# A two-layer diffusion backbone on one core: modulation sums and rotary products moved to PSUM, the third token part started later, and another layout for the second attention's keys and queries

## The chip, the cores and the metric

The kernel runs on one core of one Trainium2 chip. The metric is the device time of one execution in microseconds (us). A core has five engines with a queue of instructions each: TensorE (matmul; in the profile PE, and PEld for its weight loads), VectorE (DVE), ScalarE (ACT), GpSimd (POOL) and SyncE (SP), which here issues nearly all DMA transfers. Matmuls write to PSUM, which has eight banks of 128 partitions x 512 floats. In the profile, "L237" is line 237 of the kernel.

## The reference

There are 1024 latent tokens and 256 context tokens of width 1024, and two layers. For each layer, a conditioning vector gives shift, scale and gate (the modulation), once for the latent tokens and once for the context:

```
m = silu(cond) @ w + b                      # (1024) @ (1024 x 3072): shift, scale, gate
h = rms_norm(x, norm_g) * (1 + scale) + shift
x = x + gate * mixer(h)
```

The first layer's mixer has two attentions with eight query heads and two key heads each: A is global, with an RMS norm of queries and keys; B has a window of 128 tokens on either side and a sink per head. The queries and keys of the latent tokens are rotated in both:

```
x1, x2 = x[0::2], x[1::2]
out = interleave(x1 * cos - x2 * sin, x1 * sin + x2 * cos)
```

The second layer's mixer has a convolution over tokens (31 taps, with gates and a layer norm) and the second attention D: eight heads, each query looking at a neighbourhood in a 16 x 64 grid with a table of biases, and at the context. Every mixer ends in a projection of width 1024, and the result is a final RMS norm of the latent tokens.

## The kernel before

**Precision.** Values are split into a high and a low part, and each product is three matmuls (`mm3`: high x high, high x low, low x high, L337 to L339). The splitting is `split`: a cast on ScalarE (L315) and a subtraction on GpSimd or VectorE (L318).

**Tokens.** They come in three parts, `CHUNKS`: the 256 context tokens, and two parts of 512 latent ones. In the projections they are ten blocks of 128, of which blocks 0 and 1 are context, 2 to 5 the second part and 6 to 9 the third part.

**Opening.** A string, `PLAN`, gives the order by hand. Its letters are pieces of work: `a`, `b`, `c` quarter steps of modulation halves on TensorE (`mod_half`), `v` and `V` one half on VectorE (`mod_half_v`), digits the loads of a token part, `w` weights, `n` the sum of squares of the next token part (`norm_x`), `r` the broadcast of its inverse root (`norm_bc`), `H` and `h` the making of the normed and modulated h (`h_part`, which runs `make_h`, L325 to L331). In the string, the third part's `n`, `r`, `h` are the last three letters. Work in the opening is placed while `solo` is true, and then `bank` hands out projection banks in turn from two tags, `pp` and `mx`, of two banks each.

**The rest of the modulation.** The matrices of the first layer's gate and all of the second layer's are too many for the plan. They are done in halves of 512 columns by `mod_half_v`, in the background: the generator `mods` goes one step on at each `tick`, which `proj_qkv` and `proj_gate` call three times in a block of projections. A step loads or takes a slice `w` of 128 x 512 weights and adds `w` x conditioning to one sum per condition (L232 for the first product, L237 for the others; eight products per half). At the end, TensorE sums over the partitions (L243, tile `trm`) and VectorE adds the bias (L244). While `solo` holds, all products are on VectorE; later ScalarE and GpSimd do some. The background work has a lower priority (`LATE`).

**First attention's projections.** `proj_qkv(u, w)` makes four query heads, a key head and a value head for one of four head groups: u of 0 and 1 belong to A, 2 and 3 to B. The groups run in the order 2, 3, 0, 1. It goes through five pairs of blocks. Each block's 24 matmuls fill a bank of 384 columns, `pq`: 320 of queries and keys and 64 of values. ScalarE copies it to `pc` (L849). After two blocks, for A the norm follows, then the values are split and stored (L865 to L867), and the pair is rotated (L873 twice and L875 on VectorE, L877 on GpSimd). `qk_tail` then transposes a block (L885, tile `trk`), splits it (`qs`) and stores it. `proj_gate` makes the gate path. The first group (u of 2) runs alone, the next ones are woven in between the tiles of the attention of the group ahead.

**Second layer.** `d_proj(i)` projects for the head pair i of attention D: queries, keys, values and gate. Queries and keys are stored to `QD` and `KD` in DRAM in a high and a low part, with 128 partitions that hold two heads of 64. `load_head` and `load_q` bring them back for one head: the keys as high part on partitions 0 to 63 and low part on 64 to 127 of `KAt`, the queries as high part twice in `QH` and low part in `QL`. These loads, the bias tables (`bm`, `bs`), values (`Vt`) and the weights (`wr`, L348) share SP's queue. `d_proj(0)` runs beside the convolution, `d_proj(1)` beside the layer norm, and `d_proj(2)` and `d_proj(3)` are woven into attention D.

The order on each engine's queue is set when the program is built, by priorities in the order of the program and a model of the time; in the run each queue keeps its order and waits for semaphores.

Of the kernel before, what the change touches and what calls it, by code (L numbers as in the profile page):

```python
# [10 lines left out]
F32 = mybir.dt.float32  # L11
# [7 lines left out]
P = 128  # L19
# [34 lines left out]
PCB = 3  # L54
MODP = ((), (1, 3, 6))
# [26 lines left out]
PLAN = 'pavaa0vabvnabbvabrbbwcVHcccw1Ch2nrhnrh'  # L82
# [14 lines left out]
def tile_kernel(ctx: ExitStack, tc: tile.TileContext, a, out):  # L97
# [11 lines left out]
    mk, mwp, hold, layer = [0], [None], [0], [0]  # L109
    sts, pvs = [], []  # L110

    def bank(tag, name):
        if tag == "pp" and solo[0]:
            turn[0] += 1
            tag = ("pp", "mx")[turn[0] // 2 % 2]
        return ps.tile([P, 512], F32, tag=tag, name=name, bufs=BUFS[tag])
# [93 lines left out]
    def mod_half_v(pool, l, part, j, conds):  # L210
# [3 lines left out]
        accs = [pool.tile([P, 512], F32, tag=tag, name=nm("macc"), bufs=bufs) for _ in conds]  # L214
        pre = []
        for dk in range(DK):
# [13 lines left out]
            for q, t in zip(conds, accs):  # L230
                if dk == 0:
                    VE.tensor_scalar(t, w, csil[:, dk, q : q + 1], None, op0=ALU.mult)  # L232
                elif dk in MODP[q] and not solo[0]:
                    SC.activation(w, w, AF.Identity, scale=csil[:, dk, q : q + 1])
                    GP.tensor_tensor(t, t, w, op=ALU.add)
                else:
                    VE.scalar_tensor_tensor(t, w, csil[:, dk, q : q + 1], t, op0=ALU.mult, op1=ALU.add)  # L237
# [139 lines left out]
    def load_k(k, ks):  # L377
        KA, KB = Ks[k % len(Ks)]
        for s_ in range(2):
            SY.dma_start(KA[s_ * 64 : (s_ + 1) * 64, :].bitcast(F32), ks[:, s_])  # L380
        return KA, KB
# [299 lines left out]
    with ExitStack() as p0x:  # L681
# [6 lines left out]
        with tc.tile_pool(name="st0", bufs=1, reuse_waits="tile") as st0:  # L688
# [31 lines left out]
            def norm_bc(c, acc):  # L720
                n = CHUNKS[c][1]
                return run(rstd_steps(st0, [acc], n, "st"))[:, :n]
# [11 lines left out]
            for ev in PLAN:  # L734
# [24 lines left out]
                elif ev == "r":  # L759
                    bcs.append(norm_bc(len(bcs), accs[len(bcs)]))  # L760
# [6 lines left out]
            mwp[0] = None  # L767
        ap = p0x.enter_context(tc.tile_pool(name="p0", bufs=1, reuse_waits="tile"))
# [12 lines left out]

        tails = []
# [52 lines left out]

        def proj_qkv(u, w):
            wh, wl = w or load_w0("ev_qkv", u, 384)
            for jp in range(5):
                pc = ap.tile([P, 2, 384], F32, tag="pc", name=nm("pc"), bufs=PCB)
                for jj in range(2):  # L840
                    j = 2 * jp + jj
                    pp = bank("pp", nm("pq"))
# [6 lines left out]
                    SC.copy(pc[:, jj, :], pp[:, 0:384])  # L849
# [3 lines left out]
                t2 = ap.tile([P, 2, 5, 64], F32, tag="rt2", name=nm("rt2"), bufs=2)  # L853
                if u < 2:
                    SC.activation(t2, p5, AF.Square)
# [12 lines left out]
                if jp > 0:  # L868
# [52 lines left out]
        solo[0] = False  # L921
# [26 lines left out]
    QD = [dram(f"QD{i}", [P, 2, 2, 512]) for i in range(4)]  # L948
    KD = [dram(f"KD{i}", [P, 2, 12 * P]) for i in range(4)]
# [196 lines left out]
    with ExitStack():  # L1146
# [77 lines left out]
        def d_proj(i):  # L1224
            wsrc = (wp, WB)
            wh, wl = load_w(wsrc[0], a["od_d"], i * 512, 256, 256, wsrc[1])
            for c in (1, 2):
# [8 lines left out]
                for s_ in range(2):  # L1236
                    SY.dma_start(QD[i][:, s_, :, o : o + 256],
                                 sp[:, s_, :].rearrange("p (h q) -> p h q", h=2).bitcast(F32))
            for c in (1, 2, 0):
                t0, n = CHUNKS[c]  # L1240
                pp = yield from proj1(wh, wl, 1, c)
                if c == 0:
                    sp = pair("spk")
                    split(pp[:, :n], sp[:, 0, :n], sp[:, 1, :n], "s", "v")
                    SY.dma_start(KD[i][:, :, 0:n], sp[:, :, :n].bitcast(F32))
# [6 lines left out]
                if c == 2:  # L1252
                    for s_ in range(2):
                        SY.dma_start(KD[i][:, s_, 256:], sk2[:, s_, :].bitcast(F32))
# [74 lines left out]
        def load_head(hd):  # L1329
            i, e = divmod(hd, 2)  # L1330
            ds = slice(e * 64, (e + 1) * 64)
            heads[hd] = load_k(hd, KD[i][ds])

        def group1(gi, hd, hf):
# [4 lines left out]
            def load_q(QH, QL):  # L1339
                SY.dma_start(QH[0:64, :].bitcast(F32), QD[i][ds, 0, hf])  # L1340
                SY.dma_start(QH[64:128, :].bitcast(F32), QD[i][ds, 0, hf])
                SY.dma_start(QL[0:64, :].bitcast(F32), QD[i][ds, 1, hf])
# [381 lines left out]
```

## Time and profile before

| | |
|---|---|
| median of 3 runs | 1522.37 us (1521.3 to 1523.64) |
| profiled execution | 1517.21 us, span 1515.3 us |
| mean granted TensorE clock | 0.978 |
| busy TensorE, VectorE, GpSimd, ScalarE | 95%, 72%, 54%, 50% |
| DMA | 213.15 MB, mean 141 GB/s |

The profile is of one execution. The span is from its first to its last instruction. A busy time is the time in which an engine executed at least one instruction; a wait is idle time of an engine, put down to the instruction or transfer that ended it. The granted clock is the TensorE clock relative to full speed. Windows give these in stretches of the span. The stages by time are: the opening with the first group's projections, to about 140; projections woven into the first attention, to about 500; the attention with the first output projection, to about 880; the convolution with the second layer's first projections, to about 1105; then the layer norm and attention D, and the end from about 1450.

### The profile page before, as it was taken

The page shows a single profiled execution, that of the slowest core. Times are in us where ns is not written, and L with a number is a line of the kernel's source. Part 1 is how long each engine was busy: PE and PEld are TensorE (multiplying, and loading weights), DVE is VectorE, ACT ScalarE, POOL GpSimd, SP SyncE. Part 2 cuts the span into 40 slices and gives each one's busy share as a digit, 9 for nine tenths or more (in the row PEclk, how much of TensorE's full clock was granted, in tenths as well). Part 3 has the DMA queues.
Part 4 walks back from the last instruction along what each step waited for, and adds up shares of the span by engine and source line. Part 5 has one row for each costly group of instructions (what it writes and reads, how often), then busy time and mean ns, then how long its engine had stood idle before and what let it go on. Part 6 is the DMA issues. An engine that isn't in the chain of part 4 may idle for free. (4 is left out here: it accounts for less than half of the span.)

```text
span 1515.3 us, 22054 instructions
## 1 busy us (share of the span) xinstructions
PE 1435.6 (95%) x7054; PEld 1169.1 (77%) x7054; DVE 1094.9 (72%) x2096; ACT 757.0 (50%) x1541; POOL 821.0 (54%) x757
## 2 busy tenths in 40 slices
PE   7879989999999999999999989999999999999997
PEld 2879967886789678778888768888778878878777
DVE  5899898589957667555477775999936667668764
ACT  3721354445453666665445664543434355555563
POOL 3361464365645686776545665755543333354665
PEclk9999999999999999999999989999999999999998
DMA  9558235523541123652111112312395667788723
GB/s 350 207 174 253 75 120 171 156 66 98 170 140 59 38 81 116 197 169 63 43 45 46 60 53 87 93 59 80 130 313 188 215 189 207 242 264 234 196 68 112
DMA packets 180588, 213.15 MB, mean 141 GB/s; under 512 B 17004, under 2 KB 133944, under 8 KB 180472
## 3 DMA queue, kind: packets, MB, share of 16 engines
q1 hardware_dynamic: 173808, 200.16, 42.2%
q10 hardware_dynamic: 6664, 11.57, 2.4%
q8 instruction: 56, 0.92, 0.2%
q14 instruction: 60, 0.49, 0.1%
HBM read 151.64 MB, written 60.03 MB: 140 GB/s over the span
## 5 line engine op out<-in xcount | busy, mean ns | idle before, releaser
L318 POOL TENSOR_TENSOR pl<-pf,ph 128x512 fp32r<-128x512 f32 (+3 forms) x321 | 391.3, 1229 | 277.4 <-ACT ph L315 227.6
L318 POOL TENSOR_TENSOR wl<-wr,wh 128x256 fp32r<-128x256 f32 (+2 forms) x253 | 194.2, 785 | 141.5 <-ACT wh L315 113.8
L506 ACT ACTIVATE pf<-st 128x512 f32<-128x512 f32 x284 | 167.4, 597 | 178.5 <-PE st L498 127.4
L315 ACT CAST ph<-pf 128x512 fp32r<-128x512 f32 (+3 forms) x364 | 205.9, 578 | 24.9 <-PE ov L437 12.8
L337 PE MATMUL p<-hh,wh 128*128 128x512 f32 x448 | 178.1, 400 | 0.7 <-ACT wh L315 0.7
L339 PE MATMUL p<-hh,wl 128*128 128x512 f32 x448 | 175.0, 399 | 3.1 <-POOL wl L318 3.0
L338 PE MATMUL p<-hl,wh 128*128 128x512 f32 x448 | 176.2, 395 | 0.0
L315 ACT CAST wh<-wr 128x256 fp32r<-128x256 f32 (+2 forms) x260 | 102.0, 404 | 132.9 <-DMA wr<-in_od_d_dram 29.4
L436 PE MATMUL ov<-ph,Vt 128*128 128x512 f32 (+3 forms) x364 | 142.2, 391 | 13.3 <-DVE y L660 8.2
L494 PE MATMUL st<-QH,KAt 128*128 128x512 f32 (+3 forms) x364 | 140.0, 386 | 13.2 <-ACT pf L506 9.6
L438 PE MATMUL ov<-pl,Vt 128*128 128x512 f32 (+3 forms) x364 | 142.3, 392 | 4.7 <-POOL pl L318 2.7
L437 PE MATMUL ov<-ph,Vt 128*64 128x512 f32 (+3 forms) x364 | 139.3, 383 | 0.0
L498 PE MATMUL st<-QL,KBt 68*128 68x512 f32 (+3 forms) x364 | 134.6, 379 | 0.3 <-DVE QL L407 0.3
L1163 DVE SCALAR_TENSOR_TENSOR cps<-U,taps,cps 128x512 f32<-128x512 f32 x184 | 124.3, 749 | 0.0
L618 DVE TENSOR_REDUCE mp<-mx 128x1 f32<-128x512 f32 x128 | 85.5, 684 | 37.9 <-PE mx L617 37.2
L237 DVE SCALAR_TENSOR_TENSOR macc<-mw,csil,macc 128x512 f32<-128x512 f32 x107 | 95.6, 913 | 21.1 <-DMA mw<-in_mod_w_dram 20.1
L339 PEld LDWEIGHTS p<-hh,wl 128*128 128x128 f32 x448 | 84.6, 189 | 24.6 <-POOL wl L318 3.6
L337 PEld LDWEIGHTS p<-hh,wh 128*128 128x128 f32 x448 | 84.5, 189 | 19.1 <-ACT wh L315 0.9
L338 PEld LDWEIGHTS p<-hl,wh 128*128 128x128 f32 x448 | 84.6, 189 | 18.4
L436 PEld LDWEIGHTS ov<-ph,Vt 128*128 128x128 f32 x364 | 71.3, 196 | 30.9 <-issue 7.1
L438 PEld LDWEIGHTS ov<-pl,Vt 128*128 128x128 f32 x364 | 71.0, 195 | 30.5 <-POOL pl L318 7.7
L494 PEld LDWEIGHTS st<-QH,KAt 128*128 128x128 f32 x364 | 68.9, 190 | 31.1 <-ACT pf L506 15.6
(270 smaller groups left out, 3487.9 us busy)
## 6 DMA issues: line engine op xcount, KB each, us to landing
mw<-in_mod_w_dram SPq DMA_DIRECT2D x34, 512.0 KB, 5.8
Q<-qs SPq DMA_DIRECT2D x40, 256.0 KB, 2.5
QH<-Q SPq DMA_DIRECT2D x80, 128.0 KB, 2.8
bm<-in_d_bm_dram SPq DMA_DIRECT2D x16, 540.0 KB, 5.5
wr<-in_od_d_dram SPq DMA_DIRECT2D x64, 128.0 KB, 2.9
mw<-in_mod_w_dram SPq DMA_DIRECT2D x28, 256.0 KB, 3.1
wr<-in_ev_qkv_dram SPq DMA_DIRECT2D x32, 192.0 KB, 3.6
KAt<-KD SPq DMA_DIRECT2D x16, 384.0 KB, 6.2
```

The lines of the kernel that those rows point to most:

```text
L315: SC.copy(hi, src)
L318: (GP if leng == "g" else VE).tensor_tensor(lo, src, hi.bitcast(F32), op=ALU.subtract)
L337: PE.matmul(o, lh, rh, start=first, stop=False)
L338: PE.matmul(o, lh, rl, start=False, stop=False)
L339: done[0] = PE.matmul(o, ll, rh, start=False, stop=last)
L436: PE.matmul(o, V[:, 64:192], ph, start=(t == 0), stop=False)
L437: PE.matmul(cut(g.ov[0:64], q0, n), V[:, 0:64], ph, start=False, stop=False)
L438: pvs.append(PE.matmul(o, V[:, 64:192], pl, start=False, stop=(last and g.sink is None)))
L494: sts.append(PE.matmul(sf, KA[:, cs], cut(g.QH, q0, n), start=True, stop=False))
L498: PE.matmul(sf, KB[0:68, cs], cut(g.QL[0:68], q0, n), start=False, stop=True)
L506: SC.activation(pf[:, :n], st[:, :n], AF.Exp, scale=1.0 if g.bias else SCALE)
L1163: VE.scalar_tensor_tensor(pc, uc, w, pc, op0=ALU.mult, op1=ALU.add)
```

## The change

- `mod_half_v` puts the running sums of the first four halves of the background modulation (`PSH`) into PSUM banks of the tag `mx`, one per condition. The last of the eight products reads the bank and writes the sum in SBUF. While these may be used, the new flag `sums` keeps the projections on the two `pp` banks.
- The third token part's three steps leave `PLAN` and are run inside the first group's `proj_qkv`: `n` ahead of block 0, `r` ahead of block 2, `h` ahead of block 3 (`LASTN`).
- For the groups of B, blocks 2 to 9 are rotated one by one in a new function `rope`, which reads the projection's bank in place of a copy; ScalarE copies only the 64 value columns.
- `QD` and `KD` hold each head's parts in the order in which they are needed on 128 partitions, with the high part of the queries stored twice. Loading takes fewer transfers, storing takes more.

```
 PCB = 3
+PSH = 4
...
-PLAN = 'pavaa0vabvnabbvabrbbwcVHcccw1Ch2nrhnrh'
+PLAN = 'pavaa0vabvnabbvabrbbwcVHcccw1Ch2nrh'
+LASTN = (0, 2, 3)
...
+    sums, made_v = [False], [0]
...
-        if tag == "pp" and solo[0]:
+        if tag == "pp" and solo[0] and not sums[0]:
...
         accs = [pool.tile([P, 512], F32, tag=tag, name=nm("macc"), bufs=bufs) for _ in conds]
+        runs = accs
+        if mwp[0] is None:
+            made_v[0] += 1
+            if made_v[0] <= PSH:
+                runs = [ps.tile([P, 512], F32, tag="mx", name=nm("mrun"), bufs=BUFS["mx"]) for _ in conds]
...
-            for q, t in zip(conds, accs):
+            for q, t, r_ in zip(conds, accs, runs):
                 if dk == 0:
-                    VE.tensor_scalar(t, w, csil[:, dk, q : q + 1], None, op0=ALU.mult)
+                    VE.tensor_scalar(r_, w, csil[:, dk, q : q + 1], None, op0=ALU.mult)
...
-                    VE.scalar_tensor_tensor(t, w, csil[:, dk, q : q + 1], t, op0=ALU.mult, op1=ALU.add)
+                    VE.scalar_tensor_tensor(t if dk == DK - 1 else r_, w, csil[:, dk, q : q + 1], r_, op0=ALU.mult, op1=ALU.add)
...
         KA, KB = Ks[k % len(Ks)]
-        for s_ in range(2):
-            SY.dma_start(KA[s_ * 64 : (s_ + 1) * 64, :].bitcast(F32), ks[:, s_])
+        SY.dma_start(KA.bitcast(F32), ks)
...
             mwp[0] = None
+            sums[0] = True
...
+        third = [lambda: accs.append(norm_x(2)), lambda: bcs.append(norm_bc(2, accs[2], ap)), lambda: h_part(range(DK))]
...
+        def rope(pp, pc, jp, jj):
+
+            j = 2 * jp - 2 + jj
+            t2 = ap.tile([P, 640], F32, tag="rt2", name=nm("rt"), bufs=2)[:, 0:320].rearrange("p (h d) -> p h d", d=64)
+            s4 = pp[:, 0:320].rearrange("p (h i two) -> p h i two", two=2, i=32)
+            d4 = t2.rearrange("p h (i two) -> p h i two", two=2)
+            k4 = kcs[:, 1, j, :].rearrange("p (i two) -> p i two", two=2)
+            for e in range(2):
+                VE.tensor_tensor(d4[:, :, :, e], s4[:, :, :, 1 - e], k4[:, None, :, e].broadcast_to([P, 5, 32]), op=ALU.mult)
+            p5 = pc[:, jj, 0:320].rearrange("p (h d) -> p h d", d=64)
+            VE.tensor_tensor(p5, pp[:, 0:320].rearrange("p (h d) -> p h d", d=64),
+                             kcs[:, 0, j, None, :].broadcast_to([P, 5, 64]), op=ALU.mult)
+            SC.copy(pc[:, jj, 320:384], pp[:, 320:384])
+            GP.tensor_tensor(p5, p5, t2, op=ALU.add)
+
         def proj_qkv(u, w):
             wh, wl = w or load_w0("ev_qkv", u, 384)
             for jp in range(5):
+                if w:
+                    for k_, step in enumerate(third):
+                        if LASTN[k_] == 2 * jp:
+                            step()
...
                     j = 2 * jp + jj
+                    if w and jj:
+                        for k_, step in enumerate(third):
+                            if LASTN[k_] == 2 * jp + 1:
+                                step()
...
-                    SC.copy(pc[:, jj, :], pp[:, 0:384])
+                    if u < 2 or jp == 0:
+                        SC.copy(pc[:, jj, :], pp[:, 0:384])
+                    else:
+                        rope(pp, pc, jp, jj)
...
-                if jp > 0:
+                if jp > 0 and u < 2:
...
-        solo[0] = False
+        solo[0] = sums[0] = False
...
-    QD = [dram(f"QD{i}", [P, 2, 2, 512]) for i in range(4)]
-    KD = [dram(f"KD{i}", [P, 2, 12 * P]) for i in range(4)]
+    QD = [dram(f"QD{i}", [2, 192, 2, 512]) for i in range(4)]
+    KD = [dram(f"KD{i}", [2, P, 12 * P]) for i in range(4)]
...
-                for s_ in range(2):
-                    SY.dma_start(QD[i][:, s_, :, o : o + 256],
-                                 sp[:, s_, :].rearrange("p (h q) -> p h q", h=2).bitcast(F32))
+                for e in range(2):
+                    es = slice(e * 64, (e + 1) * 64)
+                    for k, s_ in enumerate((0, 0, 1)):
+                        SY.dma_start(QD[i][e, k * 64 : (k + 1) * 64, :, o : o + 256],
+                                     sp[es, s_, :].rearrange("p (h q) -> p h q", h=2).bitcast(F32))
...
-                    SY.dma_start(KD[i][:, :, 0:n], sp[:, :, :n].bitcast(F32))
+                    for e in range(2):
+                        SY.dma_start(KD[i][e].rearrange("(s d) n -> d s n", s=2)[:, :, 0:n],
+                                     sp[e * 64 : (e + 1) * 64, :, :n].bitcast(F32))
...
-                    for s_ in range(2):
-                        SY.dma_start(KD[i][:, s_, 256:], sk2[:, s_, :].bitcast(F32))
+                    for e in range(2):
+                        SY.dma_start(KD[i][e].rearrange("(s d) n -> d s n", s=2)[:, :, 256:],
+                                     sk2[e * 64 : (e + 1) * 64, :, :].bitcast(F32))
...
-            heads[hd] = load_k(hd, KD[i][ds])
+            heads[hd] = load_k(hd, KD[i][e])
...
-                SY.dma_start(QH[0:64, :].bitcast(F32), QD[i][ds, 0, hf])
-                SY.dma_start(QH[64:128, :].bitcast(F32), QD[i][ds, 0, hf])
-                SY.dma_start(QL[0:64, :].bitcast(F32), QD[i][ds, 1, hf])
+                SY.dma_start(QH.bitcast(F32), QD[i][e, 0:128, hf])
+                SY.dma_start(QL[0:64, :].bitcast(F32), QD[i][e, 128:192, hf])
```

More of the change, by code (lines that the diff above doesn't have):

```diff
@@ L718, in norm_x, with norm_bc @@
                 return acc
-            def norm_bc(c, acc):
+            def norm_bc(c, acc, pool):
                 n = CHUNKS[c][1]
-                return run(rstd_steps(st0, [acc], n, "st"))[:, :n]
+                return run(rstd_steps(pool, [acc], n, "st"))[:, :n]
             made = [0]
@@ L759, in tile_kernel @@
                 elif ev == "r":
-                    bcs.append(norm_bc(len(bcs), accs[len(bcs)]))
+                    bcs.append(norm_bc(len(bcs), accs[len(bcs)], st0))
                 elif ev == "H":
@@ L852, in proj_qkv @@
                 p5 = pc[:, :, 0:320].rearrange("p j (h d) -> p j h d", d=64)
-                t2 = ap.tile([P, 2, 5, 64], F32, tag="rt2", name=nm("rt2"), bufs=2)
                 if u < 2:
+                    t2 = ap.tile([P, 2, 5, 64], F32, tag="rt2", name=nm("rt2"), bufs=2)
                     SC.activation(t2, p5, AF.Square)
```

## The prediction

> **What bounds the kernel now.** I read the page's engine shares first, then busy time in slices of 5 us over the opening, then what TensorE waits for there, then the durations of VectorE's sums, and last the second attention's waits and transfers.
>
> ```profile
> PE 1435.6 (95%) x7054; PEld 1169.1 (77%) x7054; DVE 1094.9 (72%) x2096; ACT 757.0 (50%) x1541; POOL 821.0 (54%) x757
> ```
>
> TensorE is the bound: only 79.7 of 1515.3 us are not matmul, so an edit is worth the TensorE gaps that it closes. Where are they? The windows' columns are the stretch, its length, busy time of PE, PEld, DVE, ACT, POOL, granted clock, DMA share, GB/s.
>
> ```profile
> 80.00:85.00 5.00, 3.37 (x20) 2.76 (x19) 5.00 (x5) 0.62 (x1) 5.00 (x4) 1.00 0.24 71
> 85.00:90.00 5.00, 3.36 (x21) 3.00 (x20) 5.00 (x7) 1.76 (x4) 2.81 (x3) 1.00 0.57 184
> 90.00:95.00 5.00, 3.95 (x24) 3.66 (x23) 5.00 (x4) 1.88 (x5) 4.75 (x5) 1.00 0.47 134
> 95.00:100.00 5.00, 3.74 (x23) 3.22 (x22) 5.00 (x9) 1.30 (x3) 1.16 (x1) 1.00 0.58 171
> 100.00:105.00 5.00, 4.24 (x28) 4.25 (x29) 3.11 (x4) 0.30 (x1) 4.36 (x3) 0.79 0.89 246
> 105.00:110.00 5.00, 3.71 (x21) 2.91 (x20) 4.27 (x8) 1.46 (x5) 2.62 (x3) 0.84 0.92 288
> 110.00:115.00 5.00, 5.00 (x16) 3.91 (x16) 5.00 (x9) 1.37 (x3) 2.45 (x2) 0.69 0.61 181
> ```
>
> From 80 to 100 VectorE is busy without a break and TensorE is not; after it the clock falls for 15 us. TensorE's waits from 78 to 109 name VectorE in every row (total, times, longest):
>
> ```profile
> PE trk L885 <- DVE qs L318: 5.8, 5, 1.6
> PE trm L243 <- DVE macc L237: 0.9, 1, 0.9
> PE pq L339 <- DVE hl L329: 0.9, 1, 0.9
> ```
>
> Together 7.6 us. Why VectorE is late shows in the order of time:
>
> ```profile
> 88.97 1.84 POOL L318 TENSOR_TENSOR gl<-gr,gh 128x512 fp32r<-128x512 f32 x1 [2.19 <-ACT gh L315]
> 89.57 3.76 DVE L237 SCALAR_TENSOR_TENSOR macc<-mw,csil,macc 128x512 f32<-128x512 f32 x2
> 90.77 2.02 POOL L877 TENSOR_TENSOR pc<-pc,rt 128x640 f32<-128x640 f32 x1
> ...
> 98.57 0.74 DVE L237 SCALAR_TENSOR_TENSOR macc<-mw,csil,macc 128x512 f32<-128x512 f32 x1
> ```
>
> One sum takes 0.74 us when GpSimd is idle; two took 3.76 while GpSimd worked. The same operation elsewhere, with its running sum in PSUM (L1163, the convolution), and here with it in SBUF (L237):
>
> ```profile
> L1163 DVE SCALAR_TENSOR_TENSOR cps<-U,taps,cps x184: 743/749/752, 946.8 to 1100.6; 128x512 f32<-128x512 f32 x184
> L237 DVE SCALAR_TENSOR_TENSOR macc<-mw,csil,macc x107: 731/750/2054, 7.6 to 443.4; 128x512 f32<-128x512 f32 x107
> ```
>
> Shortest, median, longest: 743/749/752 ns against 731/750/2054. The medians are equal, only the tail differs. VectorE's groups from 70 to 112 (busy us, mean ns):
>
> ```profile
> L237 DVE SCALAR_TENSOR_TENSOR macc<-mw,csil,macc 128x512 f32<-128x512 f32 x17 | 20.7, 1233 | 0.0
> L873 DVE TENSOR_TENSOR rt<-pc,k_cs 128x320 f32<-128x320 f32 x8 | 5.6, 738 | 2.6 <-ACT pc L849 2.6
> L329 DVE SCALAR_TENSOR_TENSOR hl<-xr,modT,hh 128x512 fp32r<-128x512 f32 x4 | 5.2, 1327 | 0.0
> ...
> L875 DVE TENSOR_TENSOR pc<-pc,k_cs 128x640 f32<-128x640 f32 x4 | 3.2, 812 | 0.0
> L232 DVE TENSOR_SCALAR macc<-mw,csil 128x512 f32<-128x512 f32 x3 | 3.2, 1093 | 0.0
> ```
>
> **1. Sums in PSUM.** The first four halves after the opening's plan keep their two sums in the `mx` banks; seven of eight products of each write PSUM, the last reads PSUM and writes SBUF. At L1163's mean of 0.749, the 17 sums of 70 to 112 cost 12.7 us in place of 20.7, and three first products 2.2 in place of 3.2 (a first product in the bank priced as a sum; ends -1 and +1). VectorE gets 9 us back in a stretch where TensorE lost 7.6 to it.
>
> **2. Rotations from PSUM.** In two of the four head groups (u of 2 and 3), for blocks 2 to 9, ScalarE's copy of 384 columns shrinks to 64, and VectorE reads the projection's bank with two products of 160 and one of 320 columns per block, in place of two of 320 and one of 640 per pair. Nearest rows, one operand in PSUM and one in SBUF (by shape, whole kernel):
>
> ```profile
> L503 DVE TENSOR_TENSOR pf<-st,bs 128x256 f32<-128x256 f32 x32 | 13.4, 418 | 7.9 <-PE st L498 6.4 <-POOL pl L318 1.3
> L503 DVE TENSOR_TENSOR pf<-st,bs 128x128 f32<-128x128 f32 x16 | 4.6, 285 | 6.7 <-PE st L498 2.9 <-POOL pl L318 1.4 <-PE ov L438 1.3
> ```
>
> 133 ns per 128 columns gives 0.32 and 0.48: 1.12 us per block, 2.24 per pair, against 2 x 0.738 + 0.812 = 2.29 before. For VectorE this is even: 0, ends -2 (the four pairs at no contention) and +2 us. GpSimd has two additions of 320 for one of 640: one fixed part more, off the path.
>
> What it adds is a coupling. The bank is now free only when VectorE is through, not after a ScalarE copy, and the opening's projections have two banks in place of four, since `mx` holds the sums. One block's matmuls, first and last of 24:
>
> ```profile
> 65.46 0.42 PE L337 MATMUL pq<-wh,hh 128*128 128x384 f32 x1
> ...
> 69.54 0.34 PE L339 MATMUL pq<-wh,hl 128*128 128x384 f32 x1
> ```
>
> 4.2 us. With two banks the rotation must be over within one block. Behind two sums it ends 1.5 + 1.1 = 2.6 us after the block; a transpose's eviction ahead of it makes some 3.1 us. That fits, with 1 us to spare. I take +1 us for the blocks where it does not, ends 0 and +5 (the 5.8 us that TensorE now waits on VectorE for the transposes, most of it back under another name).
>
> **3. Third part later.** Norm, broadcast and h of the last 512 tokens, 16 + 8 + 8 VectorE and ScalarE operations on the norm and the h chain, move from before all projections to before blocks 0, 2 and 3. Nothing is added; no transfer moves (x of that part is loaded as before). Rows:
>
> ```profile
> 65.74 5.36 DVE L325 SCALAR_TENSOR_TENSOR xr<-xr,gs,bc 128x512 f32<-128x512 f32 x8 [3.21 <-PE bc L280]
> ...
> 81.67 0.44 PE L339 MATMUL pq<-wh,hl 128*128 128x384 f32 x1 [0.87 <-DVE hl L329]
> ```
>
> VectorE idles 3.2 us before this part, and TensorE waits 0.9 for its last pieces. Sums of the modulation can now come in front of it and fill the idle time, or push it back. I take 0; ends -3.2 (the idle time used) and +9 (rival D).
>
> **4. Clock.** From 100 to 115 the granted clock is 0.79, 0.84, 0.69: (0.21 + 0.16 + 0.31) x 5 = 3.4 us of lost matmul time right behind the 20 us in which TensorE was busy 72%. I let it shrink with the gaps.
> The Trainium skill's page "TensorE: Matmul & The Clock Gate", Part 1 (the clock gate), says that the clock falls after an idle window of about 3.4 us. The longest wait here is 1.6 us, so a reading of that rule by single gaps would not tie this fall to these waits. The windows show the fall behind a stretch of many short gaps; the same page's passage on micro-idling between matmul groups would allow that, and no run so far tells which. Without this tie the sum below is 2.5 us smaller.
>
> **5. Second attention.** Keys are loaded with one transfer on 128 partitions for two on 64, queries with two for three: 8 + 16 issues fewer. Stores: per head pair, queries go out in 12 transfers of 64 partitions for 4 of 128, context keys in 2 for 1: 36 more. Issues rise by 12. TensorE's waits from 1130 to 1500, the landing times (KB, median us) and the queue at one of the stores:
>
> ```profile
> PE p L339 <- POOL wl L318: 3.0, 1, 3.0
> PE mx L1383 <- DMA QH<-QD: 1.7, 2, 0.9
> ...
> PE mx L1383 <- DMA KAt<-KD: 0.5, 1, 0.5
> ```
> ```profile
> KAt<-KD SPq DMA_DIRECT2D x16, 384.0 KB, 6.2
> bs<-in_d_bs_dram SPq DMA_DIRECT2D x16, 384.0 KB, 3.7
> ```
> ```profile
> 1123.27 3.87 SPq L1237 DMA_DIRECT2D QD<-spq  x4
> 1130.65 0.35 SPq L348 DMA_DIRECT2D wr<-in_od_d_dram  x1
> ```
>
> 384 KB on 64 partitions take 6.2 us, on 128 partitions 3.7, so the loads should land sooner, but TensorE waited only 2.2 us for them in all: -2.2 is the end on that side. Behind the stores on SP's queue stand weight loads, and a weight's split held TensorE 3.0 us just there. At a pitch near 0.37 us (the second of these rows issues in 0.35) eight more issues hold the queue 3 us; SP stood idle from 1127.1 to 1130.7, which covers it once. I take +0.7 for the rest: -1.5 together, ends -2.2 and +7 (rival C).
>
> **Sum.** Of the 7.6 us 2.0 stay, since VectorE still has work in every slice (L329's 1.33 us sums have both operands in SBUF and stay slow): -5.6. Clock, in the same proportion, -2.5. Banks +1.0. Third part 0. Second attention -1.5. Behind the opening the transfers of the modulation's weights come nearer to the path; VectorE's waits from 110 to 180 have
>
> ```profile
> DVE macc L237 <- DMA mw<-in_mod_w_dram: 4.4, 4, 1.7
> ```
>
> and a faster VectorE runs into these more: I give back 1.5, ends 0 and 5. Total -7.1 us. The profiled execution took 1517.21 us (span 1515.3 and 1.9 around it): 1510.1, a factor 0.9953. The median of the runs is 1522.37, 0.34% above the profiled one; the factor on it gives 1515.2.
>
> **Rivals.** About 0.2% (3 us) is what a measurement of this kernel can tell from no change.
>
> A, more: all 7.6 and 3.4 go, and the first attention, now started with VectorE less behind, closes its own gap. The row is
>
> ```profile
> 180.00:200.00 20.00, 16.78 (x73) 11.72 (x72) 17.68 (x38) 10.41 (x24) 11.68 (x10) 0.83 0.20 61
> ```
>
> 3.2 us idle and 0.17 x 20 = 3.4 of clock. Half of these with the rest: -7.6 - 3.4 + 1 - 1.5 - 3.3 = -14.8, 1507.5. For it: the gap lies where VectorE is at 17.7 of 20. Against: that is softmax work the change leaves alone. Chance 0.16.
>
> B, the clock is not tied to the short gaps: -4.6, 1517.8. For it speaks only that each gap is short. Chance 0.08. (This is also what the clock page's rule by single windows gives.)
>
> C, no change: second attention's stores. At three of the four head pairs, 8 issues x 0.37 = 3 us go on the queue ahead of weight loads that TensorE then waits for, 9 us less the 2.2 gained: +6.8, with the opening's -5.6: +1.2, 1523.6; with one of the three hidden 1520.6. For it: the 3.0 us wait above, and a DMA share over 1 at the first of these places:
>
> ```profile
> 1120.00:1140.00 20.00, 17.03 (x86) 14.14 (x85) 6.44 (x13) 9.36 (x17) 5.87 (x7) 0.91 1.02 328
> ```
>
> Against: most weight loads there wait for a free buffer, not for the queue. It decides from two exposed places on. Chance 0.18.
>
> The Trainium skill's page "SBUF — State Buffer", section "Door 1: The DMA port swizzle", speaks against these stores: a transfer on 64 partitions reaches half of the ports. The 6.2 against 3.7 us above agree for loads; no row shows such a store of queries.
>
> D, slower: the third part comes too late. Its h work stands behind three blocks' ticks, nine of them, 18 sums x 0.749 = 13.5 us of VectorE. If the queue's order puts these first, h starts 12 us later; block 6 needs it some 3 us after the present start, so TensorE stands 9 us and then runs 3.4 us' worth of slow clock: -7.1 + 12.4 = +5.3, 1527.7. For it: TensorE waits for this part already (0.87 us). Against: VectorE idles 3.2 us right before it, and the ticks' work is put back in the order. From 7 us of delay on it eats the whole gain. Chance 0.16.
>
> **Numbers.** The forecast 1515.2 has 0.42, with its own range 1510 to 1519.3. Faster: all but 0.02 of it, A and B less 0.02: 0.62. Same: those 0.04 and most of C: 0.20. Slower: D and a rest of C: 0.18. For 8 in 10, half of A and half of D stay outside: 1506 to 1527.
>
> **What will show it.** From 80 to 100 TensorE above 18 of 20 and the trk waits under 2 us; modulation sums at 0.74 to 0.76 us in every case; a clock of 1.00 from 100 to 115; block 6 without a wait for h; no `pq` matmul that waits for the rotation; key loads at 768 KB landing in under 8.5 us; TensorE idle from 1100 to 1500 lower by 1 to 2 us. Wrong would be: waits on L329 or on the rotation in the opening, weight loads landing later behind the query stores, or an opening that ends early and an attention that starts when it did.

## The result, and the profile after

The changed kernel is faster: 1511.04 us against 1522.91 (medians of 18 runs each), ratio 0.9922 with a 95% interval of 0.9904 to 0.9940, about 12 us. A second measurement of the same two gave 0.9913 (0.9879 to 0.9947). The forecast was 1515.2, a factor of 0.9953. The total is inside its range, but the runs below show that it was not made up as the sum said.

The first profiled execution of the changed kernel took 1520.2 us (span 1518.4), 9 us above its median; that of the kernel before lay 5.7 us below its own. So stages are compared with a second profile of each. Engines of the changed kernel:

```profile
PE 1436.4 (95%) x7054; PEld 1175.0 (77%) x7054; DVE 1082.4 (71%) x2120; ACT 751.0 (49%) x1541; POOL 817.2 (54%) x765
```

TensorE is still the bound. The windows of its opening, with the columns of the windows in the prediction:

```profile
50.00:55.00 5.00, 0.43 (x4) 0.23 (x3) 5.00 (x9) 2.60 (x5) 0.64 (x1) 0.88 1.05 356
55.00:60.00 5.00, 0.00 (x0) 0.00 (x0) 5.00 (x9) 4.97 (x10) 3.35 (x4) 0.50 0.32 84
60.00:65.00 5.00, 1.61 (x8) 1.64 (x8) 5.00 (x8) 0.72 (x3) 2.54 (x2) 0.50 0.75 238
65.00:70.00 5.00, 5.00 (x17) 5.00 (x17) 5.00 (x10) 0.00 (x0) 1.01 (x1) 0.50 0.63 160
80.00:85.00 5.00, 5.00 (x35) 4.92 (x35) 5.00 (x9) 3.86 (x9) 3.27 (x4) 1.00 0.35 105
85.00:90.00 5.00, 5.00 (x31) 5.00 (x30) 5.00 (x13) 0.83 (x2) 5.00 (x5) 1.00 0.41 135
90.00:95.00 5.00, 5.00 (x33) 4.96 (x32) 5.00 (x11) 1.37 (x4) 1.89 (x3) 1.00 0.87 261
95.00:100.00 5.00, 5.00 (x34) 5.00 (x32) 5.00 (x11) 1.24 (x4) 3.43 (x4) 1.00 0.76 243
100.00:105.00 5.00, 5.00 (x36) 4.96 (x35) 5.00 (x11) 2.13 (x5) 1.31 (x2) 1.00 0.90 262
105.00:110.00 5.00, 5.00 (x38) 4.97 (x38) 4.40 (x10) 0.67 (x2) 3.44 (x4) 1.00 0.93 286
```

From 80 to 110 every gap is gone and the clock is full, more than was forecast. But there is a new hole from 50.4 to 63.4, and half the clock up to 70. The kernel before, in the first three of these windows:

```profile
50.00:55.00 5.00, 2.51 (x8) 2.29 (x9) 5.00 (x8) 4.45 (x8) 2.49 (x2) 0.67 1.07 357
55.00:60.00 5.00, 5.00 (x21) 5.00 (x20) 5.00 (x7) 3.55 (x7) 3.22 (x3) 0.65 0.10 32
60.00:65.00 5.00, 5.00 (x35) 5.00 (x34) 1.60 (x4) 0.63 (x2) 1.01 (x1) 1.00 0.61 193
```

The changed kernel in the order of time:

```profile
49.06 1.40 DVE L240 TENSOR_SCALAR mrun<-mw,csil 128x512 f32<-128x512 f32 x2
...
59.57 0.85 ACT L882 COPY pc<-pq 128x384 f32<-128x384 f32 x2
62.56 0.68 DVE L724 TENSOR_TENSOR acc<-acc,sq 128x512 f32<-128x512 f32 x1
63.39 1.84 PE L277 MATMUL trs<-ones,acc 128*128 128x2 f32 x8 [12.96 <-DVE acc L724]
```

Two projection banks are in use, and ScalarE copies blocks 0 and 1 out of them only at 59.57, behind its work for h. Block 2 has no bank, and ahead of it on TensorE's queue stands the third part's `trs`, which waits for the norm's sums, between which VectorE takes modulation sums. The copies end at 60.4, so the last 3 us of the hole are the wait of `trs`. Block 2 starts at 65.1 us; before, at 52.5.

A smaller gap follows at 111 us. TensorE waits 1.97 us there (2.50 in the second profile) for a projection bank, for the copy of the 64 value columns, which stands on ScalarE's queue behind a cast of weights that have not landed:

```profile
112.45 0.51 ACT L323 CAST wh<-wr 128x384 fp32r<-128x384 f32 x1 [1.71 <-DMA wr<-in_ev_qkv_dram]
112.87 0.20 ACT L857 COPY pc<-pq 128x64 f32<-128x64 f32 x1
...
113.13 0.51 PE L345 MATMUL pg<-hh,gh 128*128 128x512 f32 x1 [1.97 <-ACT pc L857]
```

And the gap at the first attention's start, the row of the prediction's rival A (16.78 of 20 us busy, clock 0.83), is closed:

```profile
180.00:200.00 20.00, 19.42 (x109) 17.30 (x108) 18.96 (x41) 8.78 (x22) 11.13 (x10) 1.00 0.22 66
```

VectorE's sums (shortest, median, longest) are as forecast:

```profile
L245 DVE SCALAR_TENSOR_TENSOR macc<-mw,csil,macc x51: 739/751/2155, 7.7 to 439.5; 128x512 f32<-128x512 f32 x51
L245 DVE SCALAR_TENSOR_TENSOR mrun<-mw,csil,mrun x48: 734/745/754, 51.0 to 128.7; 128x512 f32<-128x512 f32 x48
```

In the bank none of 48 is stretched; in SBUF the longest still takes 2.155 us. The Trainium skill's page "SBUF — State Buffer", section "Summary: rules for kernel authors", has VectorE with two SBUF inputs and GpSimd's SBUF reads block each other, whichever comes second; these two rows agree with it.

### The profile page after: what moved, and what is told of

Same layout as the page of the kernel before. It is cut to its first block, busy times and chain, and to the rows that moved or that the text cites. A ratio compares the mean times of both kernels' runs of the same rounds, so it can differ in the third digit from the quotient of the medians.

```text
span 1518.4 us, 22121 instructions
## 1 busy us (share of the span) xinstructions
PE 1436.4 (95%) x7054; PEld 1175.0 (77%) x7054; DVE 1082.4 (71%) x2120; ACT 751.0 (49%) x1541; POOL 817.2 (54%) x765
## 4 chain that ended last, share of the span: by engine, by line
PE 69%; DVE 11%; DMA 11%; issue 3%; POOL 2%; SPq 2%; ACT 2%; DVEq 0%; POOLq 0%; ACTq 0%
PE p L345 5%; PE p L346 5%; PE p L347 5%; PE ov L443 4%; PE ov L445 4%; PE po L345 4%; PE ov L444 4%; PE po L347 4%; PE po L346 4%; PE st L505 4%; PE st L501 4%; DMA mw<-in_mod_w_dram 3%; PE pq L345 3%; PE pq L346 2%; PE pq L347 2%
## 5 line engine op out<-in xcount | busy, mean ns | idle before, releaser
L445 PE MATMUL ov<-pl,Vt 128*128 128x512 f32 (+3 forms) x364 | 141.5, 390 | 4.2 <-POOL pl L326 2.3
L345 PE MATMUL pq<-wh,hh 128*128 128x384 f32 x256 | 88.9, 347 | 0.5 <-ACT pc L857 0.5
L347 PE MATMUL pq<-wh,hl 128*128 128x384 f32 x256 | 88.5, 346 | 0.0
```

Of the source, the lines that this page charges most:

```text
L345: PE.matmul(o, lh, rh, start=first, stop=False)
L347: done[0] = PE.matmul(o, ll, rh, start=False, stop=last)
L445: pvs.append(PE.matmul(o, V[:, 64:192], pl, start=False, stop=(last and g.sink is None)))
```

## The experiments

Nine kernels take parts of the change away or do parts alone, one adds the banks' restriction without its use, and two are the kernels themselves again. For each, the table has the ratio to the kernel before, and of its one profile, in us: the start of block 2, of the first scores (`st`), of the 31st matmul into `ov` (scores times values), and of the first into `p` (the second layer), with the stretch between the last two, "the first attention". "Order" is worked out from the traces: TensorE's matmuls from the first scores to the first `p`, as the sequence of tiles that they write (repeats merged, 1,124 to 1,186 steps); the longest common subsequence with the changed kernel's, as a share of the longer.

| kernel | ratio (95%) | block 2 | scores | ov 31 | p | first attention | order |
|---|---|---|---|---|---|---|---|
| before | 1 | 52.5 | 155.6 | 206.9 | 909.1 | 702.2 | 0.93 |
| before_again | 0.9994 (0.9970–1.0018) | 52.6 | 155.7 | 206.9 | 905.8 | 698.9 | 0.93 |
| changed | 0.9922 (0.9904–0.9940) | 65.1 | 142.5 | 201.4 | 903.7 | 702.4 | 1 |
| after_again | 0.9913 (0.9879–0.9947) | 64.4 | 142.0 | 199.4 | 902.0 | 702.6 | 1.00 |
| layout_only | 0.9934 (0.9908–0.9960) | 52.8 | 155.8 | 206.6 | 905.0 | 698.4 | 0.93 |
| no_layout | 0.9966 (0.9945–0.9986) | 65.2 | 141.7 | 201.7 | 900.8 | 699.1 | 1.00 |
| sums_late | 0.9929 (0.9902–0.9956) | 52.7 | 141.5 | 196.9 | 901.2 | 704.4 | 0.95 |
| sums_only | 1.0067 (1.0045–1.0089) | 68.1 | 143.9 | 195.7 | 914.4 | 718.7 | 0.81 |
| third_back | 0.9981 (0.9955–1.0007) | 68.7 | 143.6 | 196.5 | 913.1 | 716.6 | 0.83 |
| third_44 | 1.0009 (0.9985–1.0034) | 65.1 | 146.8 | 201.1 | 914.4 | 713.3 | 0.83 |
| no_sums | 1.0056 (1.0035–1.0077) | 52.6 | 154.7 | 207.9 | 918.6 | 710.7 | 0.82 |
| banks_only | 1.0016 (0.9997–1.0035) | 62.6 | 147.9 | 203.3 | 917.5 | 714.2 | 0.83 |
| late_third_back | 0.9977 (0.9954–1.0000) | 52.5 | 146.6 | 204.3 | 914.5 | 710.2 | 0.83 |
| no_rope | 1.0044 (1.0022–1.0066) | 64.3 | 144.0 | 200.8 | 914.4 | 713.6 | 0.83 |

Only the first `p` marks the same amount of work in all of them: 4,180 matmuls stand ahead of it. Ahead of the first scores there are 677 in the kernel before, 589 in the changed one and 654 in no_sums, and ahead of the 31st `ov` 913, 898 and 905 (860 in sums_only, 862 in third_back). So an earlier "scores" or "ov 31" is in part only less work ahead of it. "Like for like" below means corrected for these matmuls, at 0.17 to 0.23 us each for projections and scores and 0.11 for the others, spacings read from the traces: an estimate.

At first there were two theories: 1, VectorE's relief by the PSUM sums is the gain (the prediction's); 2, the two banks cost what the sums bring. (The recorded expectations number their own theories anew each time.)

**sums_only: the kernel before with the sums and the two banks alone.**

```
+            if made_v[0] <= PSH:
+                runs = [ps.tile([P, 512], F32, tag="mx", name=nm("mrun"), bufs=BUFS["mx"]) for _ in conds]
...
-        if tag == "pp" and solo[0]:
+        if tag == "pp" and solo[0] and not sums[0]:
```

> The kernel before with only the running sums of four modulation halves in PSUM (and two projection banks while they are there); rotations from the copy, the third part in the plan, the old layout. Theory 1 (the gain is VectorE's time behind GpSimd in the opening): trk waits from 78 to 109 fall from 5.8 to under 2 us, TensorE busy above 19 of 20 from 80 to 100, and 1514 to 1516 us, ratio 0.995 to 0.996. Theory 2 (most of the gain is in the second attention's loads): the opening is shorter but the end moves by under 3 us, ratio 0.998 or above. Theory 3 (the sums alone do not help, since the rotations and their copies still wait behind GpSimd): trk waits stay above 4 us.

Slower by 0.67%. Where theory 1 looked it was right: from 80 to 115 TensorE is busy without a break. But the hole is there too (a wait of 13.0 us), and the first `p` comes 7 us later than before. Theory 1 cannot stand as it was: the part that was to carry the gain costs time when alone.

**layout_only: the kernel before with the new layout alone.**

```
+    QD = [dram(f"QD{i}", [2, 192, 2, 512]) for i in range(4)]
+    KD = [dram(f"KD{i}", [2, P, 12 * P]) for i in range(4)]
...
```

> The kernel before with only the new layout of the second attention's keys and queries. Theory 1: the loads land sooner, but TensorE waited only 2.2 us for them; -1.5 us, ratio 0.998 to 1.0. Theory 2: -5 us or more, ratio 0.9965 or below. The rival of the query stores: weight loads issued later at 1130, 1190 and 1285, ratio 1.001 to 1.005.

Faster by 0.66%, several times the 1.5 us of the forecast.

**third_back: the changed kernel with the third part back in `PLAN`.**

```
-PLAN = 'pavaa0vabvnabbvabrbbwcVHcccw1Ch2nrh'
+PLAN = 'pavaa0vabvnabbvabrbbwcVHcccw1Ch2nrhnrh'
```

> The changed kernel with the third token part back in the plan, ahead of all projections. In the profile of the changed kernel TensorE stood 13.0 us at the third part's sum over partitions, ahead of block 2, and ran at half clock to 71. If the move causes this: the wait goes, block 2 starts near 52 as before, and the time falls by 5 to 10 us against the changed kernel, ratio to before 0.986 to 0.989. If the sums cause it (VectorE takes them ahead of the third part's squares): the wait stays and the ratio is near 0.992.

0.59% slower than the changed kernel: moving the third part, priced at 0, is worth 9 us in this company. The hole before block 2 is there all the same (68.7), so the move does not make it.

**third_44: the third part's last two steps ahead of block 4.**

```
-LASTN = (0, 2, 3)
+LASTN = (0, 4, 4)
```

> The changed kernel with the broadcast and h of the third part both ahead of block 4, so two blocks of projections stand in front of the sum over partitions that TensorE waited 13.0 us for. If that queue position is the cause: block 2 starts at 52 to 54, no wait above 2 us at the sum, block 6 waits for h by 0 to 5 us, net 4 to 9 us faster than the changed kernel, ratio 0.986 to 0.990. If the third part is simply late on VectorE: the wait moves to block 6 and the ratio stays near 0.992.

No faster than the kernel before, and block 2 starts at 65.1 us as in the changed one. The edit did not do what the expectation counted on: the sum over partitions `trs` still stands ahead of block 2 on TensorE's queue, with the same wait of 13.0 us, so this run says nothing on its place there.

**no_sums: the changed kernel with sums in SBUF and four banks.**

```
-PSH = 4
+PSH = 0
...
-            sums[0] = True
+            sums[0] = False
```

> The changed kernel without the PSUM sums and with the four banks for projections back in the opening; rotations, later third part and second attention's layout stay. Theory 2 (the two banks cost the opening, the relief of VectorE is worth less): block 2 starts again at 52 to 54 us instead of 65.1, the 12.96 us wait of the transposed sums is gone, the waits of 80 to 110 us come back in part (3 to 8 us), and the time is 1505 to 1511 us, ratio 0.986 to 0.991. Theory 1 (the sums in PSUM are worth their relief once the third part is late): the time is above the changed kernel's, ratio 0.994 to 1.000.

Block 2 is back at 52.6 and the hole closed, as theory 2 wanted:

```profile
50.00:55.00 5.00, 2.39 (x7) 2.16 (x8) 5.00 (x8) 4.33 (x8) 2.36 (x2) 0.65 1.05 353
55.00:60.00 5.00, 5.00 (x21) 5.00 (x21) 5.00 (x7) 3.67 (x7) 3.33 (x3) 0.67 0.10 33
```

But the kernel is 1.3% slower than the changed one. Theory 2 falls too: the 31st `ov` comes at 207.9 instead of 200.4 (some 6 us later like for like), and the first attention then takes 710.7 us. From 78 to 109 us 3.3 us of waits are back, as expected.

**banks_only: the restriction to two banks, with nothing in the others.**

```
-PSH = 4
+PSH = 0
```

> The changed kernel with the modulation sums back in SBUF and nothing in the freed banks: two banks for projections are kept in the opening. It pays the restriction and gets no relief. If the restriction makes the hole, TensorE is idle from about 50 to 63 us as in the changed kernel and the waits of 80 to 110 us are back as well: 1517 to 1524 us, ratio 0.995 to 1.000, slower than the kernel without the restriction. If the hole comes from the sums' order on VectorE, block 2 starts before 56 us and the time is within 3 us of the kernel without the restriction.

```profile
50.00:55.00 5.00, 0.35 (x4) 0.16 (x2) 4.61 (x7) 3.83 (x7) 1.86 (x2) 0.87 1.06 353
55.00:60.00 5.00, 0.00 (x0) 0.00 (x0) 5.00 (x7) 4.16 (x8) 3.20 (x3) 0.50 0.08 26
60.00:65.00 5.00, 4.11 (x16) 4.14 (x17) 4.91 (x11) 0.30 (x1) 1.75 (x2) 0.50 0.57 190
```

The hole is there without any sum in PSUM, and in no_sums, which differs by the restriction alone, it is not: the restriction makes it. Yet this kernel is 0.4% faster than no_sums. So a hole at 55 us does not decide the time.

**sums_late: two banks and PSUM sums from the fifth block on.**

```
-            if made_v[0] <= PSH:
+            if 1 < made_v[0] <= PSH:
...
-            sums[0] = True
...
             for jp in range(5):
+                if w and jp == 2:
+                    sums[0] = True
```

> The changed kernel, but the restriction to two banks and the PSUM sums begin with the fifth block of keys and queries and the second pair of modulation halves, so that blocks 0 to 3 rotate over four banks. Theory 2: block 2 starts at 52 to 55 us, most of the relief of 80 to 110 us is kept (TensorE over 4.6 of 5 us in each slice), and the time is the best of the four, 1502 to 1509 us, ratio 0.984 to 0.990. Rival (the hole moves to block 4 or to the third part's columns, wherever the two banks begin): a wait of 5 us or more shows between 70 and 95 us and the ratio stays 0.990 to 0.995.

```profile
70.00:75.00 5.00, 4.37 (x26) 4.04 (x24) 5.00 (x8) 2.40 (x5) 1.31 (x2) 1.00 0.25 95
75.00:80.00 5.00, 0.52 (x3) 0.31 (x3) 5.00 (x10) 5.00 (x10) 3.73 (x3) 0.87 0.00 0
80.00:85.00 5.00, 3.41 (x12) 3.44 (x13) 5.00 (x10) 2.84 (x8) 3.94 (x4) 0.50 0.68 188
```

The rival named there was right, though its one wait of 5 us is two, of 3.6 and 3.1: a smaller hole opens at 74 us, and VectorE is busy without a break around it. So the hole was moved and made smaller, not removed. The first scores come when they did (141.5), the 31st `ov` 3.5 us earlier than in the changed kernel, and the total is the same within the intervals.

**no_layout: the changed kernel without the new layout.** The edit is layout_only's, reversed.

> The changed kernel with the second attention's keys and queries laid out as before. Theory 2 (the layout carries most of the gain, as it did alone at 0.9934): ratio 0.997 to 1.001, 1521 to 1526 us. Theory of the prediction (the layout is worth 1.5 us): ratio 0.992 to 0.995, 1513 to 1517 us.

The layout is worth 0.44% here, between the two expectations. Up to the second layer this kernel and the changed one are the same, in TensorE's order too; what differs lies behind the first `p`.

**after_again and before_again: the two kernels, unchanged.**

> The changed kernel itself once more, for a second profile: the first fell on an execution 9 us above its median. Ratio 0.990 to 0.995. If the gain sits in the first attention, from 201 to 904 us, that stretch is 695 us or less here (702.4 in the first profile, 702.2 before). If it sits behind it (the second attention), that stretch stays at 700 to 704 us and the stretch from the first gate product of the last attention to the end is 318 to 324 us instead of 329.

> The kernel before, for a second profile: the first fell on an execution 6 us below its median. Ratio 0.998 to 1.002. If its first profile was lucky in the second attention, the 321.1 us from its first exponentials to the end are 326 to 331 us here; if it was lucky in the first attention, the 702.2 us are 706 to 712 us.

The first attention repeats within 0.2 us in the one and 3.3 in the other; neither was lucky or slow there. What varies is the second attention: from its first exponentials to the end 329.5 and 322.7 us in the changed kernel, 321.2 and 329.2 in the one before. That stretch of the kernel before, first profile and second:

```profile
1194.00:1515.00 321.00, 301.22 (x1592) 252.55 (x1590) 211.65 (x507) 172.22 (x382) 160.59 (x178) 0.97 0.63 190
```
```profile
1191.00:1520.00 329.00, 307.11 (x1592) 257.07 (x1590) 213.05 (x507) 172.00 (x382) 159.44 (x178) 0.95 0.62 186
```

The same 1592 matmuls, at a granted clock of 0.97 and 0.95, with 8 us between them.

**late_third_back: sums_late, with the third part back in `PLAN`.**

```
-PLAN = 'pavaa0vabvnabbvabrbbwcVHcccw1Ch2nrh'
-LASTN = (0, 2, 3)
+PLAN = 'pavaa0vabvnabbvabrbbwcVHcccw1Ch2nrhnrh'
+LASTN = (99, 99, 99)
```

> As the kernel whose two banks and PSUM sums begin with the fifth block, but with the third part of the columns back ahead of the blocks. Theory (each of the two edits needs the other: the third part's work on VectorE beside the blocks is what fills the 52 to 80 us there, and the relief comes later): block 2 at 52 to 53 us, block 6 at 74 to 76 us instead of 82.1, no wait over 4 us between 50 and 110 us, ratio 0.983 to 0.989. Rival (taking the third part out of the start is what shortens the way to the first scores, as in the changed kernel): the first scores are at 146 us or later and the ratio is 0.994 to 1.000.

Missed: block 6 stays late (81.9 us), the first scores come at 146.6 as its rival said, and the ratio is 0.9977.

**no_rope: the changed kernel with rotations behind the copy.**

```
-                    if u < 2 or jp == 0:
+                    if True:
...
-                if jp > 0 and u < 2:
+                if jp > 0:
```

> The changed kernel with the third unit's rotations again behind the copy in SBUF, two blocks at a time. The prediction's step (the rotations cost and bring nothing, 2 us either way): ratio 0.991 to 0.994. Rival (they free the copies of ScalarE, on which the next block's bank waits): 0.995 to 0.998, and the columns projected third take longer.

1.2% slower than the changed kernel, more than either theory allowed. Up to the 31st `ov` the two are level (200.8 and 199.4 to 201.4). Some 11 of the 19 us lost are in the first attention, 713.6 against 702.5; the rest lies behind the first `p`. From 200 to 900 us, the changed kernel (second profile) and this one:

```profile
200.00:900.00 700.00, 675.11 (x3270) 545.94 (x3269) 496.24 (x946) 381.88 (x756) 429.41 (x356) 0.98 0.33 100
```
```profile
200.00:900.00 700.00, 667.35 (x3213) 537.95 (x3212) 489.79 (x927) 375.49 (x736) 421.02 (x339) 0.98 0.32 99
```

In the same 700 us it has 57 matmuls fewer on record and TensorE idles 7.8 us more. The first place is at 226 us:

```profile
226.09 1.34 DVE L245 SCALAR_TENSOR_TENSOR macc<-mw,csil,macc 128x512 f32<-128x512 f32 x1 [3.01 <-DMA mw<-in_mod_w_dram]
...
229.20 1.35 PE L612 MATMUL mx<-KAt,QH 128*128 128x256 f32 x4 [3.02 <-DVE macc L245]
```

VectorE's queue has a background modulation sum at its head whose weights have not landed, and the maxima that TensorE's next bank needs stand behind it. In the changed kernel (second profile) the same piece of modulation is taken without a wait, in another place of the queue:

```profile
226.27 1.90 DVE L245 SCALAR_TENSOR_TENSOR macc<-mw,csil,macc 128x512 f32<-128x512 f32 x2
```

**Theory 3** comes from the table's last two columns. Each queue's order is fixed when the program is built, from a model of the time, and an edit in the opening lets the whole first attention be ordered anew. The fourteen profiles fall into two groups. Seven share 93% or more of the changed kernel's order, and their first attention takes 698.4 to 704.4 us; the other seven share 81 to 83%, and it takes 710.2 to 718.7. The kernel before is in the first group, as is the whole change; every kernel with only some of the opening's edits, or with one of them altered, is in the second, but for sums_late. The means are 701.1 and 713.9; like for like (696.5 to 702.2 and 707.7 to 712.5) the groups are still apart, by some 10 us. Like for like, 8 of the 9 us that the third part's return costs are in the first attention, 12 of the rotations' 19, and 9 of the sums' 20, of which 6 come before it and 5 behind the first `p`. So a part left out costs for a good part by another order, and only the sums show a clear cost in the opening. This is an association, and over fewer cases than fourteen: the first group has only three orders (before, before_again and layout_only have the same one, and so have changed, after_again and no_layout), the second has seven, which are more like each other (87% and more) than like the first (85% at most). No run forced one kernel's order on another, and why the model's order tips was not tried.

## Why the prediction was right or wrong

**In total**, by the means of the two profiles of each: up to the 31st `ov` 200.4 us instead of 206.9, so -6.5; the first attention 702.5 instead of 700.6, +1.9; the first `p` comes 4.6 us earlier. Like for like the two are -3.9 and -0.7, since 15 matmuls have moved from the one stretch to the other. Behind the first `p` single profiles vary too much. An estimate is the median, less 1.8 us around the span, less the time of the first `p`: 613.7 us before, 606.4 after, so -7.3. The forecast had -5.6 for the opening and -1.5 for the second attention, so most of what lies beyond it is behind the first `p`.

The opening's stretches, by TensorE's idle time plus what its busy time lost to the clock, in us, before and changed (second profiles in brackets): from 48 to 80, 6.3 (6.6) and 17.4 (16.4); from 80 to 120, 11.0 (10.9) and 2.0 (4.2); from 160 to the 31st `ov`, 6.5 (6.7) and 0.6 (1.1). So the hole cost more than the relief brought, and the opening came out ahead by the gap at the first attention's start. That is rival A's added term, which had a chance of 0.16. Its reason is another one: the gap is closed or under 2 us in every kernel with two banks, banks_only too, which has no sum in PSUM, and stays with four banks throughout (before, layout_only, no_sums: 6.3 to 6.7 us). That the opening's number came near was luck.

**The relief of VectorE** was right in size: forecast 0.749 us per sum, measured 0.743 as mean of 24 between 70 and 112 us. From 0 to 200 us VectorE is busy 151.9 us instead of 161.9, in the second profiles 153.5 instead of 161.4 (forecast 9 less, for the stretch from 70 to 112). **Waits and clock** from 80 to 110: forecast 2.0 us left, measured none in the first profile, and the clock is 1.00. Rival B (a clock that the short gaps don't move) loses support by no_sums: there short gaps are back, and from 120 to 135 the granted clock is 0.68, 0.66 and 0.66 with no gap over 1.6 us ahead of it. But not every gap does it. Behind the wait at 111 us the clock stayed at 1.00 (1.97 us) and was 0.79 from 110 to 115 in the second profile (2.50 us). The Trainium skill's page "TensorE: Matmul & The Clock Gate", Part 1, has the clock halve after an idle window of about 3.4 us: the one long hole agrees (0.50 up to 70 us).

**The banks** were the step of the opening that failed. The prediction gave +1 us, at most 5, looking at blocks in steady state, where a rotation fits within one block (4.2 us there, 4.4 by the rows shown). The place was the start: ScalarE's copies of blocks 0 and 1, queued behind the h work, were not looked at, since with four banks they kept nobody waiting. The hole of 12.96 us and its clock took 11.1 us more than before from 48 to 80 us (9.8 in the second profiles). VectorE, the limit of this stretch, worked on through it (busy 29.7 of the 30 us from 50 to 80), which is a reason why the hole did not decide the time, argued and not shown; sums_late shows that a smaller and later hole brings nothing in total.

**The third part** at 0 and **the rotations** at 0 were right as prices of work, as far as the opening shows (2 us and nothing, like for like), and wrong as effects. The rotations' operations took 0.311 and 0.475 us (forecast 0.32 and 0.48), and rival D's wait for h does not show in the changed kernel. But taking the one or the other back costs 9 and 19 us, most of it in the first attention, where theory 3 puts it. No `pq` matmul waits for a rotation in the opening; the wait of 2.0 us at 111 is the coupling in another place.

```profile
L853 DVE TENSOR_TENSOR rt<-pq,k_cs 128x160 f32<-128x160 f32 x16 | 4.4, 311 | 0.3 <-PE pq L347 0.3
...
L855 DVE TENSOR_TENSOR pc<-pq,k_cs 128x320 f32<-128x320 f32 x8 | 3.8, 475 | 0.0
```

So the step behind the steps failed: the terms were added, as if each part had a price. Taken away one at a time, the four parts cost 1.34% (sums), 1.22% (rotations), 0.59% (third part) and 0.44% (layout), 3.6% together, where the whole change brings 0.8%. That the sum's total came near was luck in this too: by theory 3, this change happens to keep nearly the order that the kernel before had in the first attention (93%).

**The second attention** was mis-sized: -1.5 us, against 0.66% alone and 0.44% in company. By the estimate above, with each median put as its ratio times 1522.91 us, the nine kernels with the new layout need 603 to 613 us behind the first `p`, 607.6 in the mean, and the three with the old one (before, no_layout, sums_only) 614 to 617, 615.2 in the mean: about 8 us. That is nearly all of what the changed kernel gains there. Rival C's stores delayed nothing that shows. Loads land as forecast (KB, median us; after, from 1189 us):

```profile
KAt<-KD SPq DMA_DIRECT2D x6, 768.0 KB, 6.9
QH<-QD SPq DMA_DIRECT2D x13, 256.0 KB, 5.3
```

But TensorE's waits for queries did not shrink: 6.6 and 5.2 us in the two profiles of the changed kernel, 1.7 and 3.3 before; 5.0 in no_layout and 1.2 in layout_only, so they do not go with the layout. Its idle time from 1100 to 1500, forecast to be 1 to 2 us lower, was 17.0 and 19.0 us before and 18.9 and 17.3 after.

```profile
PE mx L1422 <- DMA QH<-QD: 6.6, 4, 4.1
```

So the layout's gain is measured, and its place is behind the first `p`, but which wait it shortens stays open: the profiles of that stretch differ among themselves by as much as it brings. The order changes there too: from the first `p` on, layout_only shares 80% of the order of the kernel before, and no_layout 79% of the changed kernel's. The nine kernels with the new layout have six different orders, so its gain does not hang on one of them; whether the transfers or the orders make it was not tried.

**The give-back** was seen, and no cost of it shows: VectorE waits 9.9 us instead of 4.4 for modulation weights from 110 to 180, and TensorE has no wait on them there.

```profile
DVE macc L245 <- DMA mw<-in_mod_w_dram: 9.9, 3, 7.1
```

No version beat the changed kernel; sums_late equals it.

## What to carry to other kernels

Where a planner orders the queues, an edit's effect is its own work plus a new order of everything behind it, and the second can be the larger: compare the order of the queues before giving a stage's time to an edit, and take a bundle apart by leaving out one part at a time as well as by doing one alone. Before times at a marker are compared, count the work ahead of it: another order moves work across it. A stall on the bounding engine can be won back later, perhaps because the engine that feeds it worked on; price it by the whole, not by its length. And a restriction on buffers is to be priced at the start of a stage, where the engine that frees them is behind, and not only in its steady state.

## What the runs showed of the hardware

One program's second attention, the same matmuls in the same order, took 321.2 and 329.2 us, with the granted clock at 0.97 and 0.95: differences of a few us in such a stage cannot be read from one profile. A key load of 768 KB on 128 partitions landed in 5.1 to 6.9 us, one of 384 KB on 64 in 5.7 to 6.4 (medians of ten profiles and of four): twice the bytes in the same time. The granted clock fell behind short gaps of TensorE, none over 1.7 us (to 0.79, 0.84 and 0.69 in the kernel before, to 0.68 and 0.66 in no_sums), and did not fall behind one of 1.97 us in the changed kernel.
